# Low weight halves of two units in seven formed by ScalarE and an adding DMA instead of by VectorE

## The chip, the cores and the metric

The kernel runs on one core of one Trainium2 chip. The metric is the device time of one launch in microseconds. Engines are named as the profile names them: PE (TensorE's matmuls), PEld (its weight loads), DVE (VectorE), ACT (ScalarE), POOL (GpSimd) and SP (the queue that issues the DMAs of the kernel before).

## What is computed

A decoder trunk of two layers over 512 tokens of 1024 features, all in float32. Every layer is a feed-forward block, a mixer and a second feed-forward block, each followed by a layer norm; the mixer of the first layer is a gated MLP, that of the second a sparse attention. The change lies in the four feed-forward blocks (`swiglu`), whose hidden width is 2816:

```python
def swiglu(x, w1, w3, w2):
    return (jax.nn.silu(x @ w1) * (x @ w3)) @ w2

for layer in range(DEPTH):                                   # DEPTH = 2
    ...
    h = post_norm(h, 0.5 * swiglu(h, ffn_w1[layer, 0], ffn_w3[layer, 0], ffn_w2[layer, 0]), ...)
    ...                                                      # mixer
    h = post_norm(h, 0.5 * swiglu(h, ffn_w1[layer, 1], ffn_w3[layer, 1], ffn_w2[layer, 1]), ...)
```

## The kernel before

TensorE multiplies in a rounded float32 (`F32R`), so each operand is kept in two parts: a high part, which is the value rounded, and a low part, which is the value less the high part. Each product is then three matmuls: high by high, low by high and high by low. `split` (line 108) makes the parts: ACT copies the source into the high tile, which rounds it, and DVE subtracts the high tile from the source and writes the low tile.

All weights of the kernel lie in DRAM as one row of units of 128x1024 (`wall`), in the order of use. `Stream` (line 113) feeds them: `load` has SP fetch unit i into a raw tile (three buffers for even units, three for odd ones), `prepare` splits the raw tile into `whi` and `wlo` (a ring of five buffers of each, `NB`), and `take` and `free` hand them to the matmuls and give them back. A raw tile is fetched anew when the last instruction that reads it has run; a ring buffer is written anew when the last matmul that reads it has run.

The up-projection of a feed-forward block (x by w1 and w3) runs, after four plain units, as ten calls of `double` (line 377). Each takes two 2x2 blocks of weights and forms the product by seven half-sized products for each of the two, from weights that are partly sums of blocks. One call takes seven units out of the ring in this order: two "first" (raw units as they are), two "sum24" and two "sum31" (sums of raw half-units that DVE forms on lines 174 to 177), and one "last", whose two halves are raw half-units. Its 14 products of 12 matmuls each run in the order p, p, q, q (the first units), p, p (sum24), r, r, p, p (sum31), r, r (sum24), p, p (last). Within a product the third matmul is the first that reads a low weight part:

```python
def product(ps, w, b, start):
    for k in range(4):
        for i, (st, mv) in enumerate(((0, 0), (0, 1), (1, 0))):   # 0: high part, 1: low part
            nc.tensor.matmul(ps, w[st][:, k, :], b[mv][:, k, :], ...)
```

So every call of `double` begins with the two "first" units, whose low parts are needed by the third matmul of its first and of its second product. A scheduler places the instructions on their engines; each engine runs its own in the order given, and waits where one is not ready. The order that it made is shown below where the change moves it.

Of the kernel before, what the change touches and what calls it, by code (L numbers as in the profile page):

```python
# [12 lines left out]
AF = mybir.ActivationFunctionType  # L13
ALU = mybir.AluOpType
# [42 lines left out]
def trunk_kernel(  # L57
# [17 lines left out]
    nc = tc.nc  # L75
# [32 lines left out]
    def split(hi, lo, src, sub=nc.vector):  # L108
        nc.scalar.activation(hi, src, AF.Copy)  # L109
        sub.tensor_tensor(lo, src, hi.bitcast(F32), op=ALU.subtract)  # L110


    class Stream:
# [46 lines left out]
        def prepare(self, i, hi, lo):  # L160
            kind, *of = self.jobs[i]
            u = of[0]
            if kind == "unit":
                for sl in (slice(0, 512), slice(512, 1024)) if i < 2 else (slice(0, 1024),):
                    split(hi[:, sl], lo[:, sl], self.raws[u][:, sl])
                self.retire(u)
                return
            half = lambda t, h: t[:, h * 512:(h + 1) * 512]
            if kind == "first":
                split(hi, lo, self.raws[u])  # L170
            elif kind == "sum24":
                a11, a12, a22, a21 = (half(self.raws[u + n], h) for n in range(2) for h in range(2))
                s31, s24 = self.spare.pop() if self.spare else self.new_sums()
                nc.vector.tensor_tensor(half(s31, 1), a22, a21, op=ALU.add)  # L174
                nc.vector.tensor_tensor(half(s24, 0), a11, half(s31, 1), op=ALU.add)
                nc.vector.tensor_tensor(half(s24, 1), a12, half(s24, 0), op=ALU.add)
                nc.vector.tensor_tensor(half(s31, 0), a11, a21, op=ALU.add)
                self.sums[u] = s31
                self.retire(u)
                split(hi, lo, s24)  # L180
            elif kind == "sum31":
                split(hi, lo, self.sums.pop(u))
            else:
                for h, j in enumerate(of):
                    split(half(hi, h), half(lo, h), half(self.raws[j + 1], 0))
                    self.retire(j + 1)

        def new_sums(self):
            return [self.sums_pool.tile([P, 1024], F32, tag="sum", name=f"sum{n}", bufs=NSUM) for n in (31, 24)]
# [835 lines left out]
```

## Time and profile before

| | |
|---|---|
| time, median of 2 runs | 2036.17 us (2036.01 to 2036.33) |
| time of the profiled execution | 2035.92 us |
| its span, first to last instruction | 2034.2 us |
| PE busy | 2009.0 us, 99% of the span |
| DVE busy | 1383.7 us, 68% |
| ACT busy | 940.5 us, 46% |
| POOL busy | 144.4 us, 7% |
| mean granted TensorE clock | 0.997 of full speed |
| moved by DMA | 221.12 MB, a mean of 109 GB/s |

The profiled execution is the one whose instructions are shown; 1.7 us of its time lie outside its span. Busy time of PE counts pipelined matmuls, so it tells that PE is not waiting for anything, not that it runs at its peak.

### The profile page before, as it was taken

The page shows a single profiled execution, that of the slowest core. Times are in us where ns is not written, and L with a number is a line of the kernel's source. Part 1 is how long each engine was busy: PE and PEld are TensorE (multiplying, and loading weights), DVE is VectorE, ACT ScalarE, POOL GpSimd, SP SyncE. Part 2 cuts the span into 40 slices and gives each one's busy share as a digit, 9 for nine tenths or more (in the row PEclk, how much of TensorE's full clock was granted, in tenths as well). Part 3 has the DMA queues.
Part 4 walks back from the last instruction along what each step waited for, and adds up shares of the span by engine and source line. Part 5 has one row for each costly group of instructions (what it writes and reads, how often), then busy time and mean ns, then how long its engine had stood idle before and what let it go on. Part 6 is the DMA issues. An engine that isn't in the chain of part 4 may idle for free.

```text
span 2034.2 us, 32073 instructions
## 1 busy us (share of the span) xinstructions
PE 2009.0 (99%) x12739; PEld 1804.4 (89%) x12739; DVE 1383.7 (68%) x2330; ACT 940.5 (46%) x1598; POOL 144.4 (7%) x249
## 2 busy tenths in 40 slices
PE   9999999999999999999999999999999999999998
PEld 7999988888789999988889999988777779999987
DVE  8888635455438978743846787536788869887534
ACT  5555532332233655532324555432678835555431
POOL 0000000000000000000000000000345500000002
PEclk9999999999999999999999999999999999999999
DMA  6332432432331232343381333432422112333421
GB/s 228 108 120 96 150 113 73 140 115 84 98 119 42 94 117 94 120 138 114 125 297 63 104 105 104 147 123 74 134 72 75 43 42 94 104 105 104 147 82 42
DMA packets 72295, 221.12 MB, mean 109 GB/s; under 512 B 8224, under 2 KB 12576, under 8 KB 72144
## 3 DMA queue, kind: packets, MB, share of 16 engines
q1 hardware_dynamic: 72144, 219.07, 32.3%
q8 instruction: 100, 1.64, 0.3%
q14 instruction: 51, 0.42, 0.1%
HBM read 212.70 MB, written 11.58 MB: 110 GB/s over the span
## 4 chain that ended last, share of the span: by engine, by line
PE 95%; ACT 2%; DVE 1%; POOL 1%; issue 0%; DMA 0%; SPq 0%; DVEq 0%; ACTq 0%; POOLq 0%
PE acc L311 30%; PE p L393 23%; PE r L393 11%; PE q L393 6%; PE pv L227 2%; PE pv L226 2%; PE pv L225 2%; PE pab L226 2%; PE pab L225 2%; PE pab L227 2%; PE pu L226 1%; PE pu L225 1%; PE pu L227 1%; PE pt L819 1%; PE po L829 1%; PE po L830 1%
## 5 line engine op out<-in xcount | busy, mean ns | idle before, releaser
L110 DVE TENSOR_TENSOR wlo<-raw,whi 128x1024 fp32r<-128x1024 f32 (+1 forms) x343 | 370.1, 1092 | 150.9 <-ACT whi L109 111.3
L109 ACT ACTIVATE whi<-raw 128x1024 fp32r<-128x1024 f32 (+1 forms) x343 | 319.9, 949 | 257.0 <-PE acc L311 58.9
L311 PE MATMUL acc<-whi,shi 128*128 128x512 f32 x800 | 260.2, 390 | 0.8 <-ACT shi L109 0.8
L311 PE MATMUL acc<-whi,slo 128*128 128x512 f32 x800 | 259.8, 390 | 0.9 <-DVE slo L110 0.9
L311 PE MATMUL acc<-wlo,shi 128*128 128x512 f32 x800 | 259.3, 389 | 0.0
L110 DVE TENSOR_TENSOR wlo<-sum,whi 128x1024 fp32r<-128x1024 f32 x160 | 194.9, 1221 | 21.4 <-ACT whi L109 21.3
L109 ACT ACTIVATE whi<-sum 128x1024 fp32r<-128x1024 f32 x160 | 168.7, 1058 | 87.6 <-PE q L393 35.7
L110 DVE TENSOR_TENSOR slo<-h,shi 128x512 fp32r<-128x512 f32 x84 | 56.4, 691 | 186.9 <-ACT shi L109 186.9
L393 PE MATMUL p<-xhi,whi 128*128 128x256 f32 x640 | 181.3, 283 | 0.0
L393 PE MATMUL p<-xhi,wlo 128*128 128x256 f32 x640 | 181.1, 283 | 0.0
L393 PE MATMUL p<-xlo,whi 128*128 128x256 f32 x640 | 181.1, 283 | 0.0
L311 PEld LDWEIGHTS acc<-whi,slo 128*128 128x128 f32 x800 | 150.1, 188 | 32.3 <-DVE slo L110 1.3
L311 PEld LDWEIGHTS acc<-whi,shi 128*128 128x128 f32 x800 | 150.1, 188 | 31.8 <-ACT shi L109 1.0
L311 PEld LDWEIGHTS acc<-wlo,shi 128*128 128x128 f32 x800 | 150.2, 188 | 31.0
L109 ACT ACTIVATE shi<-h 128x512 fp32r<-128x512 f32 x84 | 50.8, 629 | 223.9 <-PE acc L311 223.9
L253 POOL TENSOR_TENSOR rs<-ve,half_neg 128x1 f32<-128x1 f32 x28 | 27.3, 975 | 1767.0 <-DVE ve L251 1767.0
L174 DVE TENSOR_TENSOR sum<-raw 128x512 f32<-128x512 f32 x80 | 54.9, 687 | 102.0 <-DMA raw<-in_wall_dram 93.8
L393 PEld LDWEIGHTS p<-xhi,whi 128*128 128x128 f32 x640 | 122.8, 192 | 0.2
L393 PEld LDWEIGHTS p<-xlo,whi 128*128 128x128 f32 x640 | 122.9, 192 | 0.0
L393 PEld LDWEIGHTS p<-xhi,wlo 128*128 128x128 f32 x640 | 122.9, 192 | 0.0
L393 PE MATMUL q<-xlo,whi 128*128 128x256 f32 x320 | 90.6, 283 | 0.0
L393 PE MATMUL r<-xt1hi,whi 128*128 128x256 f32 x320 | 90.6, 283 | 0.0
(218 smaller groups left out, 5207.6 us busy)
## 6 DMA issues: line engine op xcount, KB each, us to landing
raw<-in_wall_dram SPq DMA_DIRECT2D x339, 512.0 KB, 3.5
gb<-in_lnp_dram SPq DMA_DIRECT2D x24, 256.0 KB, 4.2
skew_dr<-rev_dr SPq DMA_DIRECT2D x16, 320.0 KB, 7.6
cw<-in_cmp_w_dram SPq DMA_DIRECT2D x8, 512.0 KB, 5.9
k<-k_dr SPq DMA_DIRECT2D x32, 128.0 KB, 2.7
u<-skew_dr SPq DMA_DIRECT2D x16, 256.0 KB, 4.6
x_sb<-in_x_feat_dram SPq DMA_DIRECT2D x8, 256.0 KB, 5.4
x_sb<-in_x_tok_dram SPq DMA_DIRECT2D x4, 512.0 KB, 5.4
```

Of the source, the lines that this page charges most:

```text
L109: nc.scalar.activation(hi, src, AF.Copy)
L110: sub.tensor_tensor(lo, src, hi.bitcast(F32), op=ALU.subtract)
L174: nc.vector.tensor_tensor(half(s31, 1), a22, a21, op=ALU.add)
L225: nc.tensor.matmul(ps, ah, bh, start=first and i == 0, stop=False)
L226: nc.tensor.matmul(ps, ah, bl, start=False, stop=False)
L227: nc.tensor.matmul(ps, al, bh, start=False, stop=last and i == n - 1)
L253: nc.gpsimd.tensor_tensor(rs, ve, half_neg, op=ALU.pow)
L311: nc.tensor.matmul(acc[t][h], st, mv[:, h * 512:(h + 1) * 512], start=s and i == 0, stop=e and i == 2)
L393: nc.tensor.matmul(ps, w[st][:, k, :], b[mv][:, k, :], start=start and k == 0 and i == 0, stop=k == 3 and i == 2, skip_group_check=True)
L819: nc.tensor.transpose(pt[:n, hh * P:(hh + 1) * P], src, ident)
L829: nc.tensor.matmul(po, v, th, start=first, stop=False)
L830: nc.tensor.matmul(po, v, tl, start=False, stop=last)
```

## The change

For the units of kind "first" and the two halves of kind "last", the low part is made another way. ACT copies the raw tile into the high tile as before, then writes the raw tile a second time, rounded and with its sign turned, into the low tile. A DMA on GpSimd's queue then reads the same weights from DRAM once more and adds them to the low tile, so that it holds the weights less their high part. DVE has no part in it. The units of sums, the plain units, those of the down-projections and everything else keep the old `split`.

```diff
             if kind == "first":
-                split(hi, lo, self.raws[u])
+                self.split_dma(hi, lo, self.raws[u], wall[u])
...
             else:
                 for h, j in enumerate(of):
-                    split(half(hi, h), half(lo, h), half(self.raws[j + 1], 0))
+                    self.split_dma(half(hi, h), half(lo, h), half(self.raws[j + 1], 0), wall[j + 1][:, :512])
                     self.retire(j + 1)
+
+        def split_dma(self, hi, lo, raw, src):
+
+            nc.scalar.activation(hi, raw, AF.Copy)
+            nc.scalar.activation(lo, raw, AF.Copy, scale=-1.0)
+            nc.gpsimd.dma_start(out=lo, in_=src, accum_op=ALU.add)
```

The order of the matmuls within the calls of `double` stays as it was, from the second call on. Six lines are added ahead of line 188, so later lines have numbers higher by 6 in the changed kernel: L413 becomes L419, L422 becomes L428, L412 and L418 on DVE become L418 and L424.

ACT's order in one of the first calls of `double`, at the place where the "first" units (18 and 19) of the next call are split; the other calls repeat it. `h` are gate values and `sum24`, `sum31` the sums of blocks. Before:

```order
L109 ACTIVATE whi18_771<-raw12_437 128x1024
L413 ACTIVATE h4_621<-tmp_619 128x256
L109 ACTIVATE whi19_775<-raw14_565 128x1024
L109 ACTIVATE whi20_805<-sum24_808 128x1024
L413 ACTIVATE h5_622<-tmp_620 128x256
L109 ACTIVATE whi21_817<-sum24_820 128x1024
L422 ACTIVATE h4_621<-p0_613 128x256
```

And ACT's order at the same place in the changed kernel:

```order
L190 ACTIVATE whi18_779<-raw12_441 128x1024
L419 ACTIVATE h4_627<-tmp_625 128x256
L191 ACTIVATE wlo18_780<-raw12_441 128x1024
L419 ACTIVATE h5_628<-tmp_626 128x256
L190 ACTIVATE whi19_784<-raw14_571 128x1024
L191 ACTIVATE wlo19_785<-raw14_571 128x1024
L109 ACTIVATE whi20_815<-sum24_818 128x1024
L109 ACTIVATE whi21_827<-sum24_830 128x1024
L428 ACTIVATE h4_627<-p0_619 128x256
```

The negative copy of unit 18 stands between the two `h`, and both `h` and the high part of unit 19 stand ahead of the negative copy of unit 19.

DVE's order around the same place before, where `tmp` are the partial results that ACT's `h` wait for:

```order
L174 TENSOR_TENSOR sum31_819<-raw15_685 128x512
L177 TENSOR_TENSOR sum31_819<-raw14_565,raw15_685 128x512
L175 TENSOR_TENSOR sum24_820<-raw14_565,sum31_819 128x512
L412 TENSOR_TENSOR tmp_619<-tmp_619,p0_613 128x256
L176 TENSOR_TENSOR sum24_820<-raw14_565,sum24_820 128x512
L110 TENSOR_TENSOR wlo18_772<-raw12_437,whi18_771 128x1024
L412 TENSOR_TENSOR tmp_620<-tmp_620,p1_614 128x256
L110 TENSOR_TENSOR wlo19_776<-raw14_565,whi19_775 128x1024
```

And DVE's order there in the changed kernel:

```order
L174 TENSOR_TENSOR sum31_829<-raw15_693 128x512
L177 TENSOR_TENSOR sum31_829<-raw14_571,raw15_693 128x512
L175 TENSOR_TENSOR sum24_830<-raw14_571,sum31_829 128x512
L176 TENSOR_TENSOR sum24_830<-raw14_571,sum24_830 128x512
L418 TENSOR_TENSOR tmp_625<-tmp_625,p0_619 128x256
L418 TENSOR_TENSOR tmp_626<-tmp_626,p1_620 128x256
```

The two low parts are gone from DVE, and the four sums stand ahead of both `tmp`. POOL, which had no instruction in an up-projection, has these at the same place of the changed kernel:

```order
L192 DMA wlo17_686<-in_wall_dram 128x512 x2
L192 DMA wlo18_780<-in_wall_dram 128x1024
L192 DMA wlo19_785<-in_wall_dram 128x1024
L192 DMA wlo24_936<-in_wall_dram 128x512 x2
```

Each waits at the head of POOL's queue for its negative copy, in the order of the units.

## Rows read from the trace of the kernel before

**Rows 1.** The page: busy time by engine, and shares of the last chain.

```profile
PE 2009.0 (99%) x12739; PEld 1804.4 (89%) x12739; DVE 1383.7 (68%) x2330; ACT 940.5 (46%) x1598; POOL 144.4 (7%) x249
...
PE 95%; ACT 2%; DVE 1%; POOL 1%; issue 0%; DMA 0%; SPq 0%; DVEq 0%; ACTq 0%; POOLq 0%
```

**Rows 2.** Windows: the second up-projection. Busy us by engine, clock, DMA share, GB/s.

```profile
665.00:870.00 205.00, 205.00 (x1690) 203.93 (x1690) 168.18 (x244) 116.22 (x190) 0.00 (x0) 1.00 0.34 113
```

**Rows 3.** Waits of PE, whole span: us in total, times, longest.

```profile
PE po L829 <- DVE o L797: 2.6, 4, 1.2
...
PE pab L226 <- DVE xlo L110: 0.2, 1, 0.2
```

**Rows 4.** The last chain, 700 to 748 us: start, us, what.

```profile
706.73 2.88 PE q L393 x24
...
715.37 2.88 PE p L393 x24
...
721.13 5.76 PE p L393 x48
726.89 2.88 PE q L393 x24
```

**Rows 5.** Timeline of PEld: loads of the first units' low parts, start and us.

```profile
723.97 0.19 PEld L393 LDWEIGHTS p<-xhi,wlo 128*128 128x128 f32 x1
...
725.41 0.19 PEld L393 LDWEIGHTS p<-xhi,wlo 128*128 128x128 f32 x1
```

**Rows 6.** Timeline of ACT there: start, us, what, idle before and its releaser.

```profile
716.78 1.06 ACT L109 ACTIVATE whi<-raw 128x1024 fp32r<-128x1024 f32 x1 [0.98 <-PE p L393]
717.74 0.40 ACT L413 ACTIVATE h<-tmp 128x256 f32<-128x256 f32 x1
718.22 1.06 ACT L109 ACTIVATE whi<-raw 128x1024 fp32r<-128x1024 f32 x1
719.46 0.42 ACT L413 ACTIVATE h<-tmp 128x256 f32<-128x256 f32 x1 [0.18 <-DVE tmp L412]
```

**Rows 7.** Timeline of DVE there.

```profile
714.73 0.69 DVE L174 TENSOR_TENSOR sum<-raw 128x512 f32<-128x512 f32 x1 [2.73 <-DMA raw<-in_wall_dram]
...
717.27 0.41 DVE L412 TENSOR_TENSOR tmp<-tmp,p 128x256 f32<-128x256 f32 x1
717.87 1.23 DVE L110 TENSOR_TENSOR wlo<-raw,whi 128x1024 fp32r<-128x1024 f32 x1 [0.19 <-ACT whi L109]
...
719.34 1.22 DVE L110 TENSOR_TENSOR wlo<-raw,whi 128x1024 fp32r<-128x1024 f32 x1
```

**Rows 8.** Groups by line and shape: count, busy us, mean ns.

```profile
L110 DVE TENSOR_TENSOR wlo<-raw,whi 128x1024 fp32r<-128x1024 f32 x259 | 316.1, 1225 | 145.9 <-ACT whi L109 106.3 <-PE pm L516 37.9
L109 ACT ACTIVATE whi<-raw 128x1024 fp32r<-128x1024 f32 x259 | 271.3, 1054 | 241.1 <-PE acc L311 58.9 <-PE pu L226 51.6 <-PE p L393 38.4
...
L110 DVE TENSOR_TENSOR wlo<-raw,whi 128x512 fp32r<-128x512 f32 x84 | 54.1, 684 | 5.0 <-ACT whi L109 5.0
...
L109 ACT ACTIVATE whi<-raw 128x512 fp32r<-128x512 f32 x84 | 48.7, 624 | 15.9 <-PE q L393 12.0 <-DMA raw<-in_wall_dram 3.5 <-ACT whi L109 0.4
```

**Rows 9.** Line 149, 705 to 726 us: SP's issues of raw loads, and their landing.

```profile
L149 SPq DMA_DIRECT2D raw<-in_wall_dram x4: 327/328/328, 711.4 to 720.6; - x4
...
DMA to landing us min/median/max: 3.3/3.6/4.2
```

**Rows 10.** DMA queue, 665 to 870 us: packets, MB, share of 16 engines.

```profile
q1 hardware_dynamic: 6370, 22.96, 33.5%
```

**Rows 11.** Smallest instruction of POOL: mean ns, then idle before.

```profile
L253 POOL TENSOR_TENSOR rs<-ve,half_neg 128x1 f32<-128x1 f32 x28 | 27.3, 975 | 1767.0 <-DVE ve L251 1767.0
```

**Rows 12.** Issues of DMAs that read a tile of 512 KB, us to landing.

```profile
v_dr<-vv SPq DMA_DIRECT2D x4, 512.0 KB, 4.5
```

**Rows 13.** The last chain at the start of the program: one matmul slow, later fast.

```profile
9.32 0.43 PE pab L225
...
12.34 0.24 PE pab L225
```

## The prediction

> **What bounds the kernel now.** I read the page first: PE is busy 99% of the span, and 95% of the chain that ended last is PE [rows 1]. An average hides stages, so the windows came next, with one window for an up-projection, where every changed instruction lies. There PE is busy 205.00 of 205.00 us at full clock, while DVE works 168.18 us, ACT 116.22 us and POOL nothing [rows 2]. Then the waits of PE: twelve rows in the whole program, from 2.6 us down to 0.2 us [rows 3], and none of them names an instruction of `double`. So DVE, though the fuller of the two helpers, delays no matmul in the stage that is changed. A microsecond taken from DVE there can give back nothing; what counts is whether the weights still come in time.
>
> The room for that is read from the chain of one call of `double`. It is one run of products of 1.44 us each: the q pair ends the row at 706.73 us, and comes again at 726.89 us, so a call takes 20.16 us [rows 4]. The next call begins with the second half of the row at 721.13 us, and the low parts of its two first units (call them a and b) are loaded into PE at 723.97 and 725.41 us [rows 5]. The buffers for a and b come free only late in the running call: ACT's copy for a starts at 716.78 us, released by PE's p on the third pair of products from the end [rows 4, 6]. After that DVE wrote the low parts at 717.87 and 719.34 us, so they were complete at 719.10 and 720.56 us [rows 7], about 4.9 us before use. Those 4.9 us are all that the new path may spend more.
>
> **The change part by part.** DVE loses 80 subtractions of 128x1024 at 1225 ns and 80 of 128x512 at 684 ns [rows 8]: 98 + 55 = 153 us of its 1383.7, all hidden behind PE, so worth 0.
>
> ACT gains as many negative copies, which I price as its plain copies of the same shapes, 1054 and 624 ns [rows 8]: 84 + 50 = 134 us in four stages, some 34 us in each. That makes 150 of 205 us, so ACT doesn't become the bound. Its order matters more. By the starts in [rows 6] a copy holds ACT 0.96 us before the next instruction begins, and an `h` takes some 0.4 us. In the new order: high part of a from 716.78, `h` from 717.74, negative a from 718.14 to 719.20; `h` from 719.10, high part of b from 719.50, negative b from 720.46 to 721.52 us. The `h` wait for DVE's `tmp`, behind four sums that begin when a raw tile lands, at 714.73 us, and that let `tmp` start at 717.27 us [rows 7]. The raw tile is released by ACT's half-copy now instead of DVE's; I count no delay there, though the DMAs of the "last" unit share the engines with that load.
>
> So the adding DMAs of a and b can start at 719.20 and 721.52 us, and their landing is needed at 723.97 and 725.41 us: 4.77 us for a, 3.89 us for b. Those of "last" cost nothing: its buffer comes free with the q products, at 709.61 us, and it is needed in the last pair, from 721.13 us [rows 4]; less four half-copies of ACT, 2.5 us, that leaves 9 us.
>
> What such a DMA costs the trace doesn't show; POOL issues none. The nearest row is the plain load of the same 512 KB by SP: 3.3 us to landing at best, 3.6 at the median, 4.2 at worst [rows 9]. Of that, the transfer itself takes what the 16 engines give to it: 33.5% of 205 us for 22.96 MB is 1.57 us for 512 KB [rows 2, 10], which leaves 3.3 - 1.57 = 1.73 us before and after. Issue by POOL I take as its smallest instruction, 975 ns, against SP's 328 ns [rows 9, 11]: 0.65 us more. The lower end for the transfer is 1.57 us, as for a load. An adding DMA must also bring the old tile to the adder, so it moves 512 KB twice on its way in: 2 x 1.57 = 3.14 us. The upper end is 4.5 us, the whole landing time of a DMA that reads a tile of 512 KB [rows 12]. I take 3.14, since two reads are what the operation names.
>
> These DMAs aren't alone. The negative copies of a and b are the last readers of their raw tiles, so at 719.20 and 721.52 us SP issues the loads of two further units, as it did at 719.1 and 720.6 us before [rows 9]. All four then share the engines: from 719.20 us on, 1.73 + 2 x 1.57 + 2 x 3.14 = 11.15 us, which puts the landing of b at 730.35 us, 4.94 us after its need. (The engines don't run dry between: when b's data starts, some 723.1 us, a load and a's transfer, 4.7 us of work begun about 720.2, are still going.) In the next call everything hangs on PE's products again, the copy of a first of all, so the wait isn't made up but comes again in each call.
>
> **The sum.** Ten calls in each of four up-projections have 36 boundaries between them: 36 x 4.94 = 178 us. The first pair of each stage is split while plain units run; I count 0, with 4 x 4.94 = 20 us as the other end. Two of POOL's layer-norm instructions now stand behind such a DMA, at most one issue of some 1 us each, also 0. Against the profiled execution's own time, 2035.92 us, whose median differs by 0.25 us, that gives 2214 us.
>
> The Trainium skill, "DMA: Bandwidth & Descriptors" (Rules for kernel authors), says that an accumulating DMA reads its destination and writes it later. No row here shows one; by that rule the two reads stand, as the sum has them.
>
> **Rivals.**
>
> *Hidden.* If the load and the add overlap in the engines, and loads don't hold them up, a lands at 719.20 + 0.65 + 3.3 = 723.15 us, 0.8 us early, and b at 721.52 + 3.95 = 725.47 us, within 0.1 us of its need. Then nothing changes: 2036 us. For it speaks that the engines are busy only a third of the stage [rows 10]; against it, that the work comes in one burst with both raw loads. The point that decides is a landing within 3.9 us of the negative copy of b. The Trainium skill, the same page ("Anatomy of one DMA", the GpSimd path), fits 2.0 us plus bytes over 436e3; its estimate for 512 KB is 3.2 us, which is this rival, and the plain loads of 3.3 us agree with that figure, but none of them adds.
>
> *One pass.* The add costs the engines no more than a load. The four then need 1.73 + 4 x 1.57 = 8.01 us from 719.20, b lands at 727.21 us, 1.80 us late: 36 x 1.80 = 65, so 2101 us. The engines' share after would tell it from the forecast.
>
> *Heavy.* The add costs 4.5 us: 1.73 + 3.14 + 9.0 = 13.87 us, b lands at 733.07 us, 7.66 us late, and 36 x 7.66 = 276, so 2312 us. A lower clock would lead to the same place. At the start of the program, after idling, a matmul takes 0.43 us and later 0.24 us, the levels of 1.2 and 2.4 GHz [rows 13]; if each stall is followed by as long at the lower level, half of 4.94 us is lost again, 36 x 2.47 = 89 us, or 2303 us.
>
> *Gain.* The freed DVE would have to end waits of PE, of which twelve rows of at most 2.6 us exist, outside these stages [rows 3]. A gain over 2% can't come from there.
>
> **How the numbers follow.** About 2%, some 41 us, is what a measurement of this kernel can tell from no change. Forecast 0.42, one pass 0.25, heavy 0.18, hidden 0.13, gain 0.02. The predicted time is the forecast's, 2214 us. The range leaves out hidden and gain (0.15) and a little of the heavy end: from 2080 us, a b that is 1.2 us late, to 2325 us, heavy with part of the 20 us at the stages' starts. Slower by over 2% takes forecast, heavy and one pass but for a part whose b is less than 1.1 us late: 0.81. Within 2% gets that part, hidden and half of gain: 0.18. Faster gets the other half: 0.01.
>
> **What the profile after would show.** PE's p waits for a DMA named wlo at the head of each call of `double`, in all four up-projections, some 3 to 5 us in all per call, and the q rows come about 25 us apart. The DMA share of such a stage rises from a third to about 0.6 (four loads, 6.3 us, and adds of 1.5 MB, 9.4 us, in 25 us). DVE's busy time falls by 153 us and ACT's rises by 134 us, both without effect. Wrong would be: no wait of PE on wlo (hidden); waits with a share that fits plain loads (one pass); negative copies that are late themselves, because `h` or the raw tiles are, which would move the cause from DMA to ACT's order; or a long time of POOL between negative copy and first byte, which would make the issue, not the transfer, the price.

## The result

The changed kernel takes 2282.02 us (median of 2 runs, 2278.0 and 2286.03) against 2036.17 us: a ratio of 1.1207, with a 95% interval of 1.1123 to 1.1292. The forecast was 2214 us with a range of 2080 to 2325 us, so sign and range held, and the point was 68 us low.

The page of the changed kernel, busy time by engine, answers to [rows 1]; the profiled execution's span is 2284.1 us, 249.9 us more than before.

```profile
PE 2097.8 (92%) x12739; PEld 1874.7 (82%) x12739; DVE 1250.7 (55%) x2170; ACT 1037.8 (45%) x1758; POOL 284.1 (12%) x409
```

DVE has lost 133 us, and that bought nothing. PE runs the same 12739 matmuls and yet is busy 88.8 us longer. Its waits, the whole span (total us, times, longest), answer to [rows 3]:

```profile
PE p L399 <- DMA wlo<-in_wall_dram: 160.2, 65, 5.1
...
PE q L399 <- DMA wlo<-in_wall_dram: 0.9, 1, 0.9
```

Two rows that weren't there before, and both name the adding DMA. The 161.1 us of waits and the 88.8 us of longer PE work make 249.9 us: the whole difference of the spans. So two things have to be explained, the waits and the slower matmuls.

The chain of work that ended last in the fourth up-projection (start us, us, what) answers to [rows 4]:

```profile
2000.98 0.04 issue
2001.02 1.46 PE p L399 x10
2002.48 2.88 PE q L399 x24
2005.36 2.88 PE p L399 x24
2008.24 2.88 PE r L399 x24
2011.12 1.33 PE p L399 x11
2012.46 0.02 issue
2012.48 0.69 ACT whi L190
...
2013.84 0.77 ACT wlo L191
...
2015.10 0.95 ACT whi L190
2016.05 0.96 ACT wlo L191
2017.00 0.39 issue
2017.40 9.13 DMA wlo<-in_wall_dram
2026.52 0.04 issue
2026.57 2.50 PE p L399 x10
```

Before, this was PE row after PE row. Now it is a loop that goes through three engines: a product ends and frees the buffers, ACT writes the four copies for a and b, the add for b runs 9.13 us, and only then can the second product of the next call go on. The call from 2001.02 to 2026.57 us takes 25.55 us, where it took 20.16 us. The last row shows the second loss: the same ten matmuls take 2.50 us where they took 1.46 a call earlier.

The windows of the changed kernel, one for each up-projection (busy us and instructions of PE, PEld, DVE, ACT, POOL; granted clock, DMA share, GB/s), answer to [rows 2]:

```profile
25.00:270.00 245.00, 205.72 (x1549) 200.24 (x1547) 131.61 (x201) 128.12 (x209) 31.39 (x36) 0.93 0.62 148
735.00:960.00 225.00, 189.33 (x1403) 185.94 (x1403) 109.80 (x167) 112.60 (x184) 28.70 (x33) 0.89 0.58 137
1250.00:1480.00 230.00, 196.92 (x1478) 193.08 (x1478) 112.84 (x169) 117.98 (x193) 29.60 (x34) 0.90 0.59 139
1890.00:2160.00 270.00, 229.45 (x1707) 223.93 (x1707) 136.94 (x204) 140.03 (x231) 33.45 (x38) 0.91 0.59 139
```

PE stands still for 14 to 16% of each stage, and the granted clock falls from 1.00 to about 0.9. The DMA share rises from 0.34 to about 0.6, as the prediction had it.

One call in small steps, in the second up-projection (columns as above), shows the order of events:

```profile
796.00:798.00 2.00, 2.00 (x19) 2.00 (x18) 0.97 (x2) 2.00 (x3) 0.87 (x1) 1.00 0.89 225
798.00:800.00 2.00, 1.48 (x13) 1.27 (x11) 2.00 (x3) 1.42 (x3) 0.00 (x0) 1.00 0.99 166
800.00:802.00 2.00, 0.00 (x0) 0.00 (x0) 2.00 (x3) 0.55 (x2) 0.00 (x0) 1.00 1.02 285
802.00:804.00 2.00, 1.01 (x4) 1.01 (x5) 1.96 (x4) 0.00 (x0) 0.00 (x0) 0.61 1.09 233
804.00:806.00 2.00, 2.00 (x10) 1.83 (x10) 0.00 (x0) 0.38 (x1) 0.00 (x0) 0.54 0.30 57
806.00:808.00 2.00, 2.00 (x18) 2.00 (x18) 0.00 (x0) 0.38 (x1) 0.00 (x0) 1.00 0.00 0
```

The 16 DMA engines are nearly full from 796 to 804 us (the share is worked out from packet times and comes out a little over 1) while PE runs dry at 799. After 3.5 us without a matmul the clock is at 0.61 and 0.54, near the 1.2 GHz level, for some 3 us, and then at 1.00. The timeline of PE (start, us, what, wait and its releaser) shows the stall and the matmuls behind it:

```profile
799.20 0.28 PE L399 MATMUL p<-xlo,whi 128*128 128x256 f32 x1
802.99 0.58 PE L399 MATMUL p<-xhi,wlo 128*128 128x256 f32 x1 [3.51 <-DMA wlo<-in_wall_dram]
803.37 0.41 PE L399 MATMUL p<-xhi,whi 128*128 128x256 f32 x1
803.59 0.41 PE L399 MATMUL p<-xlo,whi 128*128 128x256 f32 x1
...
805.80 0.39 PE L399 MATMUL p<-xhi,wlo 128*128 128x256 f32 x1
806.03 0.28 PE L399 MATMUL p<-xhi,whi 128*128 128x256 f32 x1
806.15 0.28 PE L399 MATMUL p<-xlo,whi 128*128 128x256 f32 x1
```

Matmuls behind the stall start 0.21 us apart, at full clock 0.12 us. The stall of 802.99 us is that for a. b's low part is read first at 805.80 us, almost without a stall: b lands just then, and the time until it does has gone to the wait for a and to twelve slow matmuls. The adds of this call in POOL's timeline, and the landing of the stretch's adds:

```profile
794.68 0.89 POOL L192 DMA_DIRECT2D wlo<-in_wall_dram  x1 [6.41 <-ACT h L419]
796.88 0.87 POOL L192 DMA_DIRECT2D wlo<-in_wall_dram  x1 [1.31 <-ACT wlo L191]
...
DMA to landing us min/median/max: 7.4/8.0/8.9
```

b's add lands at 796.88 + 8.9 = 805.78 us. SP's raw load that the negative copy of a released was issued at 794.30 us, so the burst lasted 11.48 us; the prediction had 11.15.

The DMA queues of the second up-projection, 735 to 960 us (packets, MB, share of 16 engines), answer to [rows 10]:

```profile
q0 software_dynamic: 4889, 13.10, 33.6%
q1 hardware_dynamic: 4797, 17.48, 24.2%
```

q0 holds the adds: 0.336 x 225 us for 13.10 MB is 3.03 us of all engines for 512 KB. q1 holds the loads: 0.242 x 225 for 17.48 MB is 1.63 us. An add costs the engines nearly two loads.

### The profile page after: what moved, and what is told of

Read it like the earlier page. It is cut to its first block, busy times and chain, and to the rows that moved or that the text cites. A ratio compares the mean times of both kernels' runs of the same rounds, so it can differ in the third digit from the quotient of the medians.

```text
span 2284.1 us, 32628 instructions
## 1 busy us (share of the span) xinstructions
PE 2097.8 (92%) x12739; PEld 1874.7 (82%) x12739; DVE 1250.7 (55%) x2170; ACT 1037.8 (45%) x1758; POOL 284.1 (12%) x409
## 3 DMA queue, kind: packets, MB, share of 16 engines
q0 software_dynamic: 23040, 62.92, 16.1%
q8 instruction: 100, 1.64, 0.3%
## 5 line engine op out<-in xcount | busy, mean ns | idle before, releaser
L399 PE MATMUL p<-xhi,wlo 128*128 128x256 f32 x640 | 216.4, 338 | 160.4 <-DMA wlo<-in_wall_dram 160.2
L110 DVE TENSOR_TENSOR wlo<-raw,whi 128x1024 fp32r<-128x1024 f32 (+1 forms) x183 | 221.1, 1215 | 137.1 <-ACT whi L109 98.0
L399 PEld LDWEIGHTS p<-xhi,wlo 128*128 128x128 f32 x640 | 146.2, 228 | 177.6 <-DMA wlo<-in_wall_dram 177.5
L192 POOL DMA_DIRECT2D wlo<-in_wall_dram x160 | 140.0, 879 | 1037.9 <-ACT wlo L191 777.4
L399 PE MATMUL p<-xhi,whi 128*128 128x256 f32 x640 | 203.9, 319 | 0.0
L399 PE MATMUL p<-xlo,whi 128*128 128x256 f32 x640 | 203.6, 318 | 0.0
L407 DVE TENSOR_TENSOR tmp<-tmp,q 128x256 f32<-128x256 f32 x80 | 33.3, 418 | 234.3 <-PE q L399 234.3
L404 ACT ACTIVATE tmp<-p 128x256 f32<-128x256 f32 x80 | 30.7, 384 | 276.7 <-PE p L399 276.7
L399 PEld LDWEIGHTS p<-xhi,whi 128*128 128x128 f32 x640 | 146.4, 229 | 0.2 <-ACT h L437 0.2
L399 PEld LDWEIGHTS p<-xlo,whi 128*128 128x128 f32 x640 | 146.5, 229 | 0.0
```

What stands on the lines that cost most here:

```text
L192: nc.gpsimd.dma_start(out=lo, in_=src, accum_op=ALU.add)
L399: nc.tensor.matmul(ps, w[st][:, k, :], b[mv][:, k, :], start=start and k == 0 and i == 0, stop=k == 3 and i == 2, skip_group_check=True)
L404: nc.scalar.activation(tmp[s][:, 0], pp[s], AF.Copy)
L407: nc.vector.tensor_tensor(tmp[s][:, 0], tmp[s][:, 0], qq[s], op=ALU.add)
```

## The experiments

Theory: loads and adds share the 16 engines in one burst that starts with the negative copy of a; PE waits for the burst's end, and loses about half of each wait again at the lower clock. The main rivals are that an adding DMA has a long way of its own on GpSimd's queue, whatever else runs, and that the waits alone are the loss. The table gives for each run the time, its ratio to the kernel before, timed beside it, with the interval, PE's waits on `wlo`, and PE's busy time over the 2009.0 us of before.

| run | us | ratio (95%) | waits | PE busier by |
|---|---|---|---|---|
| changed kernel | 2282.0 | 1.1207 (1.1123 to 1.1292) | 161.1 | 88.8 |
| only "last" added | 2042.8 | 1.0025 (1.0016 to 1.0034) | 3.0 | 1.8 |
| only a, b added | 2282.5 | 1.1198 (1.1181 to 1.1215) | 159.1 | 88.4 |
| only a added | 2170.6 | 1.0665 (1.0645 to 1.0686) | 82.8 | 45.1 |
| only b added | 2187.2 | 1.0731 (1.0715 to 1.0747) | 94.3 | 56.3 |
| plain copies, GpSimd | 2110.5 | 1.0352 (1.0328 to 1.0376) | 54.5 | 24.3 |
| half-size adds | 2154.1 | 1.0576 (1.0558 to 1.0594) | 80.0 | 25.2 |
| short loads | 2171.1 | 1.0648 (1.0627 to 1.0670) | 96.5 | 36.6 |
| short loads, only a | 2087.2 | 1.0248 (1.0233 to 1.0263) | 32.8 | 15.7 |
| plain copies, SP | 2049.4 | 1.0064 (1.0047 to 1.0081) | 4.7 | 4.9 |
| filler matmuls | 2241.6 | 1.0995 (1.0977 to 1.1013) | 16.5 | 190.3 |
| negative copy first | 2298.3 | 1.1285 (1.1259 to 1.1310) | 166.5 | 94.2 |
| low parts last | 2194.8 | 1.0786 (1.0748 to 1.0825) | 94.2 | 65.3 |

### Which of the adds cost

Only the two halves of "last" by DMA, a and b split by DVE:

```diff
             if kind == "first":
-                self.split_dma(hi, lo, self.raws[u], wall[u])
+                split(hi, lo, self.raws[u])
```

> Only the two halves of the unit last are made by negative copy and adding DMA; the first units keep the old split. Theory: these have some 9 us until they are needed and land in about 7.5 us, so PE doesn't wait: 2034 to 2042 us. Rival (the adds slow the raw loads that they share the engines with, so that DVE's sums, ACT's h and the copies behind them are late even so): waits of PE in each call, 2060 us or more.

2042.75 us, 0.8 us over the theory's range, and far from the rival's 2060. These adds take 8.5 us to landing at the median, and PE waited for one of them a single time, 3.0 us. They cost 0.25%, since nearly always nobody needs them so soon. A slow DMA is not yet a late one.

Only a and b by DMA:

```diff
-                    self.split_dma(half(hi, h), half(lo, h), half(self.raws[j + 1], 0), wall[j + 1][:, :512])
+                    split(half(hi, h), half(lo, h), half(self.raws[j + 1], 0))
```

> Only the two first units (a and b) are made by negative copy and adding DMA; the halves of last keep the old split. Theory: the burst of two loads and two adds is the price, and it is as before, so the time stays: 2250 to 2285 us. Rival (the adds of last delay the raw loads beside them, and by those DVE's sums, ACT's h and the negative copies, and that is a large part of the cost): 2200 us or less.

2282.54 us, the changed kernel's time. The whole loss is that of a and b.

Only a, and in the other run only b, by DMA (in both, "last" by `split` as above):

```diff
             if kind == "first":
+                if self.jobs[i - 1][0] != "first":      # only a; "==" for only b
                     self.split_dma(hi, lo, self.raws[u], wall[u])
+                else:
+                    split(hi, lo, self.raws[u])
```

> Of the three changed units of a call only a, the first, gets the negative copy and the add. Theory of the burst: the negative copy ends at 718.80 us, and with it a load is issued; the landing is at 725.2 us after that load alone, 1.2 us late, and up to 726.7 us if half of the next load goes ahead too, 2.8 us late: 36 x 1.2 to 36 x 2.8 = 43 to 100 us, 2080 to 2137 us. Rival of 8.9 us from issue: 727.7, 3.7 us late, 2170 us or more.

> Of the three changed units of a call only b, the second, gets the negative copy and the add; a and last keep the old split. Theory of the burst: ACT's negative copy ends about 1.3 us earlier (720.24 us in the place read before), one load of 1.57 us is under way and another is issued with the add of 3.06 us; the landing is 0.3 us late if the add is served alone and 1.6 us late if it comes after both loads, 36 x 0.3 to 36 x 1.6 = 12 to 58 us: 2048 to 2095 us. Rival (each such DMA takes 8.9 us from issue): 720.24 + 8.9 = 729.1, 3.7 us late, 2170 us or more.

2170.6 and 2187.2 us: both outside the theory's ranges, and at or over the rival's bound. So a single add costs over half of what two cost, and the landing is why: 7.2 and 7.5 us at the median. Window and landing in the run with only a, around one call (its add was issued at 788.43 us; the landings are those of 735 to 860 us):

```profile
788.00:796.00 8.00, 5.84 (x47) 5.64 (x47) 6.82 (x10) 5.20 (x9) 0.86 (x1) 0.98 0.74 191
...
DMA to landing us min/median/max: 7.1/7.8/8.6
```

The engines did 0.74 x 8 = 5.9 us of work in this stretch. One add of 3.06 us leaves 2.9, nearly two loads of 1.57; SP issued raw loads at 788.05 and at 790.87 us. That suggests that an add issued alone still shares the engines with both raw loads. Whether they delay it, or whether 7 us is an add's own time, this run can't tell; the next group can.

### What an add costs, and what the loads beside it cost

Plain copies instead of adds, on GpSimd's queue as before (the weights' high parts are not subtracted):

```diff
-            nc.gpsimd.dma_start(out=lo, in_=src, accum_op=ALU.add)
+            nc.gpsimd.dma_start(out=lo, in_=src)
```

> The DMA on GpSimd's queue copies the weights over the low tile instead of adding them, so the low parts hold the whole weights; all else is as in the changed kernel. Theory of the engines (the add costs the 16 engines two passes, and what is late is the burst of two loads and two adds): the four transfers need 1.73 + 4 x 1.57 = 8.0 us instead of 11.2, the low part of b is some 1.8 us late, PE waits about 65 us in all for wlo, the stalls are too short for the clock to fall much, 2095 to 2115 us; the wlo DMAs of 512 KB land in 5 to 6.5 us. Rival of GpSimd's queue (such a DMA takes its 8 to 9 us from issue to landing whatever it moves, as the 8.4 us of the 256 KB ones beside 8.9 us suggest): landing and time hardly change, 2260 to 2290 us.

2110.45 us, as the theory has it. The queue took 9.3% of a span of 2112.9 us for 62.92 MB, which is 1.64 us for 512 KB, against 3.06 with the addition (16.1% of 2284.1 us, the same bytes). The landing fell from 8.9 to 5.3 us at the median. The addition doubles the engines' work, and without it 172 of the 246 us are gone.

```profile
q0 software_dynamic: 23040, 62.92, 16.1%
wlo<-in_wall_dram POOLq DMA_DIRECT2D x80, 512.0 KB, 8.9
...
q0 software_dynamic: 23040, 62.92, 9.3%
wlo<-in_wall_dram POOLq DMA_DIRECT2D x80, 512.0 KB, 5.3
```

The first two rows are the changed kernel's page (queue: packets, MB, share of 16 engines; then the issues: count, KB, median us to landing), the last two that of the plain copies.

Adds over the first half of the columns (the second half keeps the negative weights):

```diff
+            n = lo.shape[1] // 2
-            nc.gpsimd.dma_start(out=lo, in_=src, accum_op=ALU.add)
+            nc.gpsimd.dma_start(out=lo[:, :n], in_=src[:, :n], accum_op=ALU.add)
```

> Each adding DMA adds only the first half of its columns (256 KB instead of 512 KB, 128 KB instead of 256 KB), so half of each of these low parts stays the negative copy. Theory of the engines: 1.73 + 2 x 1.57 + 2 x 1.55 = 8.0 us for the burst, as with the plain copy, 2095 to 2115 us, and a landing of about 6 us for those of a and b. Rival of GpSimd's queue: 2260 to 2290 us, landing 8 us or more.

2154.11 us, between the two theories. The queue's share, 9.5% of 2148.3 us for 31.47 MB, gives 1.70 us for 256 KB, a little over half, so the burst is 1.73 + 2 x 1.57 + 2 x 1.70 = 8.27 us and b 2.06 us late: 74 us of waits, where 80 were measured. As a time it tells nothing apart, and both ranges missed. As rows it sides with the theory: the adds of a and b land after 6.1 us at the median, where the theory had about 6 and the rival 8 or more, and the wait follows the engines' work.

Loads of 256 columns instead of 1024, the adds in full:

```diff
-                    nc.sync.dma_start(raw, wall[i])
+                    n = 1024 if i < 8 else 256
+                    nc.sync.dma_start(raw[:, :n], wall[i][:, :n])
...
+            raws = {j: v(t) if j < 8 else t[:, :256].unsqueeze(1).to_broadcast([P, 4, 256]) for j, t in self.raws.items()}
```

> The changed kernel, but SP's loads of raw units fetch only the first 256 of 1024 columns of each unit (from unit 8 on), and all readers of a raw tile take these 256 columns four times: this leaves out three quarters of the weights on the loading side, while copies, matmuls, their order and the adding DMAs (full size) stay. Theory (the burst: loads and adds take turns on the 16 engines, and b lands when all of it is through): a load then takes some 0.4 to 0.5 us of the engines instead of 1.57, so from the negative copy of a on 1.73 + 2 x 0.45 + 2 x 3.06 = 8.75 us, b lands 2.5 us late instead of 4.94. The changed kernel lost 246 us for its 4.94 (waits and lower clock together); in proportion 2.5 us cost some 125 us: 2150 to 2190 us. Rival (an add has a long way of its own on GpSimd's queue, some 8.9 us from issue to landing, whatever the loads do): no less than 2250 us. If the loads alone were to blame, 2060 us or less.

2171.12 us, inside the theory's range and well under the rival's 2250. Nothing of the adds was changed, and yet they land after 6.4 us at the median instead of 8.9, and 111 us are back:

```profile
wlo<-in_wall_dram POOLq DMA_DIRECT2D x80, 512.0 KB, 6.4
```

The same with only a by DMA:

> As the run with only a by a DMA, again with loads of only 256 of 1024 columns of each raw unit (three quarters of the weights are left out on the loading side). There an add landed 7.15 us after its issue, of which, by the only add that met no load, 5.5 us are its own and the rest would be the two raw loads of 1.57 us beside it. Theory (shared engines): 5.5 plus one or two short loads of 0.45 us, so 5.7 to 6.3 us to landing, a 1.3 to 2.0 us late instead of 2.8, and in proportion to the 133 us lost there 60 to 95 us: 2098 to 2133 us. Rival (an add in use lands after some 7.2 us for a reason of its own): 2160 us or more.

2087.23 us; its landing, 735 to 960 us, and its wait:

```profile
DMA to landing us min/median/max: 5.4/5.5/5.9
...
PE p L407 <- DMA wlo<-in_wall_dram: 32.8, 36, 2.3
```

The rival falls: without long loads beside it an add lands after 5.5 us, which is 1.73 + 0.65 + 3.14 of the prediction, and the time that the first add of the changed kernel also took, at 22.1 us, where the engines were free of adds. The time is 11 us under the theory's range: the landing is below the 5.7 us with which the range began, and PE waits 0.9 us a call where the range had a 1.3 us late at the least.

### The lower clock

41 more matmuls ahead of the first product of 36 calls, whose result the product then overwrites, so that PE has work in the stall:

```diff
+        if len(hts) > 4:
+            w0 = half(first[0], 0)
+            for n in range(41):
+                nc.tensor.matmul(pp[0], w0[0][:, n % 4, :], x["b11"][0][:, n % 4, :], start=True, stop=True,
+                                 skip_group_check=True)
```

> The changed kernel with 41 more matmuls (41 x 0.12 = 4.9 us) ahead of the first product of each call of double but the first of a stage, 36 calls, 177 us of PE work; their result is overwritten by the product that follows. Theory: of the 246 us that the change cost, 161 us are waits for wlo and the rest, some 88 us, matmuls at the lower clock level after a stall; the added matmuls stand in the place of the waits and keep PE busy, so the clock stays at 1.0 and the time falls although PE does more: 2215 to 2240 us, waits for wlo under 40 us, granted clock above 0.985. Rival (the slow matmuls are not due to PE's idling, but to the DMAs or to late operands): the added matmuls come on top or leave the slow ones, 2275 us or more.

2241.62 us, 1.6 us over the theory's range: 40 us less than the changed kernel, with 1476 matmuls more. A call in 5 us steps (columns as above):

```profile
781.00:786.00 5.00, 5.00 (x44) 5.00 (x43) 1.88 (x4) 5.00 (x7) 1.76 (x2) 1.00 0.60 146
786.00:791.00 5.00, 5.00 (x44) 5.00 (x43) 5.00 (x7) 1.89 (x4) 0.00 (x0) 1.00 0.95 225
791.00:796.00 5.00, 4.28 (x36) 4.07 (x35) 1.58 (x3) 0.41 (x2) 0.00 (x0) 1.00 0.37 77
```

The clock stays at 1.00, and the mean over the run is 0.995 instead of 0.956. The 1476 fillers at 0.12 us make 177 of the 190.3 us by which PE is busier, so of the 88.8 us only 13 are left. The lower clock is therefore a price of its own, and waiting in idleness is dearer than waiting at work. But that price isn't the whole 88.8 us: fillers and waits that are left make 177 + 16.5 = 193.5 us, more than the 161.1 us of waits in the changed kernel. Up to 32 us of the slow matmuls there ran while a weight was still on its way, and at full clock PE would have waited instead.

### Order and queue

The negative copy and its add written ahead of the copy of the high part:

```diff
+            nc.scalar.activation(lo, raw, AF.Copy, scale=-1.0)
+            nc.gpsimd.dma_start(out=lo, in_=src, accum_op=ALU.add)
             nc.scalar.activation(hi, raw, AF.Copy)
-            nc.scalar.activation(lo, raw, AF.Copy, scale=-1.0)
-            nc.gpsimd.dma_start(out=lo, in_=src, accum_op=ALU.add)
```

> The changed kernel with the negative copy and its adding DMA written ahead of the copy of the high part. ACT's order then has the high part of a, h, negative a, h, negative b, high part of b: negative b ends some 1.0 us earlier, and the load that b's raw tile waits for is released by the copy of b's high part, so it is issued behind b's add instead of with it. Theory (burst): if b's load falls behind b's add, b lands after 1.73 + 1.57 + 2 x 3.06 = 9.4 us, 3.2 us late, and in proportion 246 x 3.2 / 4.94 = 160 us: 2195 us; if the engines share evenly between the queues, up to 11.0 us as before, so the expectation is 2190 to 2270 us. Rival (an add's own 8.9 us from issue to landing decides): b would land 1.0 us earlier than in the changed kernel at the most, 2230 us or more.

2298.27 us, over the theory's range: a miss, and a time that the rival's bound allows. b's add is issued 1.25 us behind a's instead of 2.20, and nothing is gained. Waits of PE in one call (adds issued at 773.33 and 774.58 us):

```profile
781.55 0.39 PE L399 MATMUL p<-xhi,wlo 128*128 128x256 f32 x1 [3.42 <-DMA wlo<-in_wall_dram]
785.03 0.58 PE L399 MATMUL p<-xhi,wlo 128*128 128x256 f32 x1 [0.86 <-DMA wlo<-in_wall_dram]
```

a is used 8.2 us and b 10.4 us after its issue, and PE waits twice in this call. So the rival's constant 8.9 us doesn't hold either: b is issued 1 us earlier and takes longer. Putting a transfer earlier into full engines didn't bring its end forward. Why the kernel became 16 us slower instead of staying equal isn't settled.

Plain copies of the same size on SP's queue, from a tile in DRAM:

```diff
-            nc.gpsimd.dma_start(out=lo, in_=src, accum_op=ALU.add)
+            if self.scratch is None:
+                self.scratch = dram.tile([P, 1024], F32, name="scratch")
...
+            nc.sync.dma_start(lo.bitcast(F32), self.scratch[:, :lo.shape[1]])
```

> The changed kernel, but in place of each adding DMA on GpSimd's queue SP issues a plain copy of the same size from a scratch tile of 512 KB in DRAM into the low tile; the correction by the weights is left out. In SP's order the copy for a stands ahead of the raw load that the same negative copy releases, and the copy for b ahead of the next raw load. The plain copies on GpSimd's queue gave 2110 us. Theory that within one queue transfers go through in the order of issue, while two queues share the engines: b's copy ends after three transfers instead of four, 0.33 + 1.73 + 3 x 1.57 = 6.8 us from the negative copy of a, so at 726.0 us at the latest, 0 to 0.6 us late: 2036 to 2065 us. Rival (all transfers in flight share the engines evenly, whichever queue they are on): four transfers as with GpSimd, b 1.8 us late: 2090 to 2115 us. If GpSimd's way of issuing were most of the price of the plain copies, the result would again be near 2036 us, but with a landing of 3.5 us at the median where the first theory has 4 to 5 us.

2049.35 us, 61 us under the plain copies on GpSimd's queue. Landings of the copies, then of the raw loads behind them, 735 to 960 us:

```profile
DMA to landing us min/median/max: 3.1/3.4/5.9
...
DMA to landing us min/median/max: 3.0/4.2/6.6
```

The copies take 3.4 us, as a load alone does; it is the raw loads that wait, at 4.3 us at the median of the whole run instead of 3.5. On GpSimd's queue it was the other way about: copies 5.3, loads 3.5. That fits a copy that gains by standing ahead of the load in the same queue. Of the 1.9 us between 5.3 and 3.4, about 0.7 can be the way of issuing (the fastest copies of 512 KB took 3.8 and 3.1 us); the rest would be the sharing. The 3.4 us were the mark for "mostly the way of issuing", so the run doesn't rule that out; the 0.7 us between the fastest and the later loads speak against it. The run also reads one scratch tile again and again instead of the weights, and no run parts this from the queue. The Trainium skill, "DMA: Bandwidth & Descriptors" (Issuing engines are not separate DMA queues), says that DMAs of all issuers run on the same 16 engines and interleave. The traces agree: two queues fill the engines together in the bursts (a share of 0.89 to 1.09 from 796 to 804 us in the changed kernel).

### A remedy

The two high-part matmuls of the first four products first, and their low-part matmuls after them, so that a and b are needed later:

```diff
-            product(pp[s], half(first[s], 0), x["b11"], True)
+            part(pp[s], half(first[s], 0), x["b11"], high, True, False)
+        for s in range(2):
+            part(qq[s], half(first[s], 1), x["b21"], high, True, False)
+        for s in range(2):
+            part(pp[s], half(first[s], 0), x["b11"], low, False, True)
...
```

> The changed kernel with another order of matmuls in the first four products of a call: the eight matmuls by high parts of each of the four first, then the four by low parts of each. The low part of a is needed at the 33rd matmul instead of the third (3.6 us later), that of b at the 37th instead of the 15th (2.6 us later). Theory: what counts is the landing of b against its need, so 2.6 us of some 5 are covered, and the stalls are too short for long stretches at the low clock: 36 x 2.3 = 83 us, 2110 to 2150 us. Rival (the loop is closed by something that this order doesn't move, such as the release of buffers or ACT's order): 2200 us or more.

2194.78 us, just under the rival's bound, and 45 us over the theory's. b's first use moves 2.6 us back (from the third matmul of the second product to the first behind 36), which leaves 2.3 of 4.94 us, 84 us of waits; 94.2 were measured. What the range missed is the clock: to the waits come 65.3 us of slower matmuls. No version here beats the kernel before, whose PE waits for nothing in these stages; of the versions that leave nothing out only the run with "last" alone equals it within 0.3%. A sixth buffer in the ring, which would free a and b earlier, was not tried.

## Why the prediction was right, and where it was short

- **What bounds the kernel** was read rightly: DVE lost 133 us (the prediction had 153), that gave back nothing, and PE now waits for weights.
- **ACT** stays off the bound (112.60 of 225 us in the second stage). Over the whole run it is busy 97 us longer, where the prediction had 134. From the start of the high part of a, the negative copies end after 2.31 and 4.51 us; the prediction's schedule had 2.42 and 4.74.
- **The price of an add**, two passes or 3.14 us, chosen between 1.57 and 4.5: measured 3.03 to 3.06. The plain copies and the share rule out one pass and the heavy price of 4.5 us. The Trainium skill, "DMA: Bandwidth & Descriptors" (Rules for kernel authors), says that an accumulate reads its destination and writes it later. The doubling from 1.64 to 3.06 us agrees with that; no trace shows the read itself.
- **The burst**: 11.15 us to b's landing, measured 11.48 in the call shown. Undoing single parts shows that loads (short loads: -111 us) and the second pass (plain copies: -172 us) both stand in it.
- **"Last" costs nothing**: its two runs show 0.25% by itself, and no difference beside a and b.
- **The sum's wait**: 36 x 4.94 = 178 us. The waits that the profile shows are 161.1 us, but the prediction counted from b's need to b's landing, and a part of that time goes to slow matmuls. By the starts of the matmuls in PE's timeline of the changed kernel (0.12 us apart at full clock), b's low part is used 200 us late in the 36 calls, 5.6 us in each. Counted in the same way, the plain copies on GpSimd's queue make b 1.9 us late in each, where *One pass* had 1.80.
- **The step that fell short** is that the sum ends at b's landing and has no term for TensorE's clock. The prediction named that loss, but under the rival *Heavy* and with half of each wait, 89 us; PE is indeed busy 88.8 us longer. The two can't simply be added to 178 us: by the same count 31 of the 200 us are slow matmuls between the first use of a and that of b, and 39 us more are slow matmuls behind b. So of the profiled execution's 249.9 us, 200 are the late b (22 more than forecast), 39 are the lower clock behind it, and the other 10 lie outside the 36 calls, most of them at the stages' starts, which the forecast counted as 0. The filler run agrees: at full clock 40 us were back. The forecast should have held this term: a stall of nearly 5 us in each call was its own result, and [rows 13] showed both levels.
- **Hidden** was refuted by 65 waits, and **gain** by the lack of any.

That PE's extra busy time is half of the wait is not a rule: it was 0.55 of the wait in the changed kernel, 0.31 with half-size adds and 0.69 with the low parts last.

## What to carry to other kernels

Work taken from an engine that nobody waits for is worth nothing, and work given to the DMA engines must be priced in the burst in which it runs, not by the stage's mean share (a third here): add up what is released by the same event, and compare the end with the first use. An adding DMA counts twice in that sum. Where the result is a stall of PE of several us, add the slow matmuls that follow the last late operand, here 39 us on top of 200, before comparing with what the edit saves.

## What the runs showed of the hardware

- An adding DMA of 512 KB into SBUF takes 3.06 us of the 16 engines, a plain one on the same queue 1.64. The adding instruction holds POOL 0.87 us, the plain one 0.53 us.
- Without long transfers beside it an add of 512 KB lands 5.5 us after its issue; in the bursts it took 8.9 us at the median.
- With adds on GpSimd's queue both queues were later (adds 8.9 us at the median, raw loads 4.2 instead of 3.5); with plain copies there the copies were (5.3 us; loads 3.5). With the copies ahead of the loads in SP's queue the copies landed after 3.4 us and the loads after 4.3.
- After 3.5 us without a matmul the granted clock was 0.61 and 0.54 in the next two windows of 2 us, then 1.00; PE kept busy with filler matmuls held 1.00.
